# One transformer block on one core: where the second output product's weights are split, and the order of the sums, first MLP weights and norm scalings behind it

## The chip, the core and the metric

The kernel runs on one core of a Trainium2 chip. The metric is the device time in microseconds of one execution. TensorE (PE) does the matmuls, VectorE (DVE), ScalarE (ACT) and GpSimd (POOL) the rest, and SyncE (SP) issues most loads. Each of them works through a queue of its own in order. An instruction that waits therefore holds up everything queued behind it on its engine.

## The reference

One block for 512 tokens of width 1024 in f32: a norm, a wide input projection, two mixers (a gated linear attention with 4 heads and a latent attention with 8), a gated sum of both, the output projection `w_out`, and an MLP of width 4096 with squared relu.

```python
n = rmsnorm(h, g_mix[l])
proj = n @ w_in[l]
...
y_gla = gla_branch(gq, gk, gv, gr, z_gf, z_gb, w_gate_f[l], b_gate_f[l], ...)
y_mla = mla_branch(cq, ckv, kr, positions, g_q[l], w_uq[l], g_kv[l], w_ukv[l])
merged = jax.nn.sigmoid(z_ma) * y_gla + jax.nn.sigmoid(z_mb) * y_mla
h = h + merged @ w_out[l]
m = rmsnorm(h, g_mlp[l])
h = h + jnp.square(jax.nn.relu(m @ w_ff1[l])) @ w_ff2[l]
...
return rmsnorm(h, g_final)
```

Within `mla_branch`, each head computes `p = softmax(q kT)` and then `p v`. This is the "attention" of the text below.

## The kernel before

**Exact products from two halves.** Every f32 operand of a matmul is held as two fp32r tiles, a high part and a low part. `split` makes them: a copy on ACT gives the high tile (names end in `h`), and a subtraction on DVE gives the low tile (names end in `l`). `mm3` then issues three matmuls, high by high, high by low and low by high (L88, L89, L90). In the trace `split` is L93 (ACT) and L94 (DVE), and `split_scaled`, which multiplies by a gain besides, is L97 and L98.

**Attention** is one loop over `n`, over 8 heads (`MH`) of 4 row tiles each, with everything staggered. In step `n`, `att_scores` makes one tile of scores `s` (three matmuls of 512 columns), its row maximum on DVE and the exponential `e` on ACT. `att_normalise` (every second step) divides two tiles by their sums, one on ACT and one on DVE (L1030). `att_flip`, three steps later, transposes a tile on PE into `tp` (four instructions of 128 columns), and splits the result into `pT` (ACT, then DVE). `att_values`, six steps later, makes half a head's values `av` out of `v` and `pT` (12 matmuls of 256 columns), and `merge` gates them. "Transposition 5.2" is head 5, row tile 2. A few loads, splits and sums for the output projection are put into the same loop by the number of the step. Two of these are `streamed(1, ..)` at n = 11, 13 and `streamed(2, ..)` at n = 21, 23. Each loads half of a block of `w_out` into a staging tile (`wf`, of which there are three) and splits it. The tiles are `bo10h`, `bo10l`, `bo11h` and so on, `bo20h`, `bo20l`, `bo21h`, `bo21l` for the second product. In the loop the framework's scheduler chooses the order on PE, ACT and DVE, with a few orders pinned by `goes_behind`.

**Output projection.** The 1024 x 1024 product is done as seven half-sized products in place of eight (a scheme of the Strassen kind), in the order 1, 2, 5, 6, 3, 7, 4. `wo_product(m)` takes the left tiles `wo_left[p][m]` (`gao`, `gdo` and others, which `split_first`, `split_sum` and `corner` make from the merged rows) and the right tiles `wo_right[m]` (`bo{m}0h` and so on, made by `split_part` from blocks `B11`, `B12`, `B21`, `B22` of `w_out`). Sums of those blocks that products 5, 6, 7 and 4 need are formed by loads that add to what lies in the tile (`load_onto`, on GpSimd's queue). Each product has 24 matmuls of 512 columns: four `p`, two row blocks `rb`, three each, except that products 3, 7 and 4 are issued in two halves, one for each `rb`. They write into three pairs of banks: `wox` (products 1, 6, 7, 4), `wow` (2) and `woz` (5, 3). Products 6, 7 and 4 go on adding to `wox`, so that `add_rows`, which adds a bank to the rows `h` on DVE (L1331), reads a bank in the middle of its sums, and the next product on that bank has to wait until it is read.

**Norm and first MLP products.** For rows 0 and 1, and later 2 and 3, `first_half_square` and `second_half_square` sum the squares on ACT, `row_rstd` makes the reciprocal root (one instruction on DVE, one on POOL, `hp`), and `scaled` multiplies the row (one half on DVE, one on ACT, both `ms`). `flipped` transposes the rows on PE, and `evacuate` brings eight banks' parts per half into `mT` (L97 on ACT, L98 on DVE). The first two MLP products `f00` and `f01` take weights that `proj_begin` loads, splits and gives a bank. They run for tokens 0 to 255 first, and after the transpositions of rows 2 and 3 for the others. `f02` follows.

**Order.** From the line `begun = traced()` ahead of the products, `in_program_order(begun, PE_ONLY + SPLITTERS)` pins PE, ACT and DVE to the order in which the program is written, up to the end of the first two MLP products. POOL is pinned so from the start of attention. SP's loads are not pinned in that way, and go where the scheduler puts them: a load waits at its place in SP's queue until the tile that it fills is free. The order of the stage that the change rewrites reads, shortened:

```python
wo_right[4] = split_w2(B21, "bo4")
wo_product(7, (0,))
add_rows(2, 1, xs_[0], ALU.subtract)
first_half_square(2, 1)
...
fm.evacuate(0, range(4))
wo_product(7, (1,), range(2, NP))
add_rows(3, 1, xs_[1], ALU.subtract)
fm.evacuate(0, range(4, KD))
...
early.append(proj_begin(w1, P, "f01", "mm"))
```

Of the kernel before, what the change touches and what calls it, by code (L numbers as in the profile page):

```python
# [18 lines left out]
P = 128  # L19
S = 512  # L20
NT = S // P
D = 1024
KD = D // P
# [33 lines left out]
def tile_block(ctx: ExitStack, tc: tile.TileContext, t, out: bass.AP):  # L57
# [34 lines left out]
    def split(hi, lo, src, rest=nc.vector):  # L92
        nc.scalar.activation(hi, src, AF.Copy)  # L93
        rest.tensor_tensor(lo, src, raw(hi), op=ALU.subtract)  # L94
# [12 lines left out]
    def traced():  # L107
        return len(nc.cur_bb.bb.instructions)
# [16 lines left out]
    def goes_behind(late, early, engines):  # L125

        ins = nc.cur_bb.bb.instructions
        for e in engines:
            a, b = [[i for i in ins[x:y] if i.engine == e] for x, y in (early, late)]
            if a and b:  # L130
                issued_after(b[0], a[-1].name)
# [48 lines left out]
    def row_rstd(parts):  # L180
        nc.vector.scalar_tensor_tensor(
            parts[:, 3:4], parts[:, 1:2], 1.0 / D, parts[:, 2:3], op0=ALU.mult, op1=ALU.add
        )
        nc.gpsimd.tensor_tensor(parts[:, 3:4], parts[:, 3:4], mhalf, op=ALU.pow)
        return parts[:, 3:4]
# [29 lines left out]
    def halves(nk, nw, name):  # L215
        wh = tl([P, nk, nw], F32R, "wh", 4, f"{name}h")
        wl = tl([P, nk, nw], F32R, "wl", 4, f"{name}l")
        return wh, wl
# [12 lines left out]
    def proj_begin(w, col, name, tag="mm"):  # L231
        wh, wl = weights(w[:, col : col + P], name)
        return wh, wl, ps(tag, name)

    def begin_late(col, name, tag="mm"):

        wf = stage(KD, P, name)
        nc.sync.dma_start(wf, w_in[:, col : col + P].rearrange("(k p) w -> p k w", p=P))
        wh, wl = halves(KD, P, name)
        nc.scalar.activation(wh, wf, AF.Copy)  # L240

        def lows():
            nc.vector.tensor_tensor(wl, wf, raw(wh), op=ALU.subtract)

        return (wh, wl, ps(tag, name)), lows
# [654 lines left out]
    def load_w2(qd, x, w=w2, block=None):  # L900

        for g, dst in enumerate(block_tiles(x)):
            for pp_ in range(2):
                nc.sync.dma_start(dst[:, pp_, :], block_rows(w, qd, x if block is None else block, g, pp_))

    def load_onto(dst, x, w):

        for g, d in enumerate(block_tiles(dst)):
            rows = w[4 * g * P : 4 * (g + 1) * P, (x % 2) * S : (x % 2 + 1) * S]
            nc.gpsimd.dma_start(d, rows.rearrange("(k t p) w -> p t k w", t=2, p=P)[:, x // 2], accum_op=ALU.add)  # L910
# [5 lines left out]
    def streamed(m, x, g):  # L916

        wf = stage(2, S, f"bo{m}{g}")
        for pp_ in range(2):
            nc.sync.dma_start(wf[:, pp_, :], block_rows(w_out, 0, x, g, pp_))  # L920
        wh, wl = halves(2, S, f"bo{m}{g}")
        split(wh, wl, wf)
        wo_right.setdefault(m, []).append((wh, wl))

    def split_part(x, g, name):
# [4 lines left out]
    def split_w2(x, name):  # L930
        return [split_part(x, g, name) for g in range(NP // 2)]
# [10 lines left out]
        eng.tensor_tensor(z[:, HT:S], a12, y[:, HT:S], op=ALU.add)  # L942
        return y, z

    merged, wo_right = {}, {}
    wo_left = [{} for _ in range(NP)]
    corners = {}

# [308 lines left out]
    next(units)  # L1257
    attending = traced()
    sums_of, flipping, span = {}, {}, {}
    for n in range(4 * MH + LAG_C):  # L1260
        if n % 2 == 0 and 2 <= n <= 4 * MH:
            att_normalise((n - 2) // 4, (n - 2) % 4)
        scored = traced()
        if n < 4 * MH:
            att_scores(n // 4, n % 4)
            if n - 2 in flipping:
                goes_behind((scored, traced()), flipping[n - 2], SPLITTERS)
        scored = scored, traced()
        if 2 <= n % 8 < 7:
            next(units, None)  # L1270
        if n in (6, 14):
            units = up_units(n // 8 + 2)
            next(units)
        b = n - LAG_B
        if 0 <= b < 4 * MH:
            flips = traced()
            att_flip(b // 4, b % 4)
            flipping[n] = flips, traced()
            if b == 0:
                gla_turn(GH - 1, (flips, traced()))  # L1280

        if n == 20:
            load_onto(B11, B12, w_out)
        extra = traced()
        for x, at in (("y", (18, 26, 34)), ("z", (20, 28, 36))):
            if n in at:
                p = at.index(n)
                to = (5, 6) if x == "y" else (7, 3)
                split_sum(wo_left[p], sums_of[p, x], *to, f"{x}o{p}", nc.gpsimd if p < 2 else nc.vector)
        if n in (19, 30):  # L1290
            p = (19, 30).index(n)
            split_first(wo_left[p], merged[p][0], f"o{p}", nc.gpsimd)
        if n < 4 * MH:
            goes_behind((extra, traced()), scored, SPLITTERS[:1])
        if n == 35:
            split_first(wo_left[2], merged[2][0], "o2")
        if n in (11, 13):
            streamed(1, B11, (n - 11) // 2)
        if n in (21, 23):
            streamed(2, B21, (n - 21) // 2)  # L1300
        if n == 15:
            load_w2(0, B11, w_out)
        if n == 17:
            at = traced()
            load_w2(0, B21, w_out, B22)
            span["sums"] = at, traced()
        if n == 23:
            load_onto(B21, B11, w_out)
        if n == 24:
            load_w2(0, B12, w_out)  # L1310
            load_w2(0, B22, w_out)
        c = n - LAG_C
        if c >= 0 and c % 2 == 1:
            att_values(c // 4, (c % 4) // 2)
        if n == 33:
            load_onto(B21, B12, w_out)
        if c > 0 and c % 8 == 7 and c // 8 < NP - 1:
            sums_of[c // 8, "y"], sums_of[c // 8, "z"] = merged_sums(c // 8, nc.gpsimd)
    load_onto(B12, B22, w_out)

    hrow = []
    for i in range(NT):
# [6 lines left out]
    def add_rows(i, c, acc, op=ALU.add):  # L1329
        hc = hrow[i][:, c * S : (c + 1) * S]  # L1330
        nc.vector.tensor_tensor(hc, hc, acc, op=op)  # L1331
# [3 lines left out]
    def first_half_square(i, c):  # L1335
        hparts[i] = sm(f"hp{i}", 4)
        ms_rows[i] = u4(f"ms{i}", F32, (P, D))
        square_half(hrow[i], c, hparts[i], ms_rows[i], True)

    def second_half_square(i, c):  # L1340
        square_half(hrow[i], c, hparts[i], ms_rows[i], False)

    def scaled(i):
        m = ms_rows[i]
        rs = row_rstd(hparts[i])
        nc.vector.tensor_scalar(m[:, 0:S], hrow[i][:, 0:S], rs, None, op0=ALU.mult)
        nc.scalar.activation(m[:, S:D], hrow[i][:, S:D], AF.Copy, scale=rs)

    def flipped(i):
        fm.rows(i, ms_rows[i])  # L1350
# [140 lines left out]
    def wo_product(m, rbs=range(2), ps_=range(NP)):  # L1491
        accs = wo_accs.get(m, xs_)
        for p in ps_:
            lh, ll = wo_left[p][m]
            wh, wl = wo_right[m][p // 2]
            for rb in rbs:
                tok = slice(rb * P, (rb + 1) * P)
                mm3(accs[rb], lh[:, tok], ll[:, tok], wh[:, p % 2, :], wl[:, p % 2, :],
                    m in (1, 2, 5) and p == 0, p == NP - 1, m not in (1, 2, 5))

    last = NP - 1
    g_last = split_first(wo_left[last], merged[last][0], f"o{last}", nc.vector, None, slice(0, HT))
    wo_product(1)
    wo_right[5] = [split_part(B11, 0, "bo5")]
    split_first(wo_left[last], merged[last][0], f"o{last}", nc.vector, g_last, slice(HT, S))
    y, z = merged_sums(last, nc.vector)
# [30 lines left out]
    for rb in range(2):  # L1537
        wo_product(3, (rb,))
        add_rows(rb, 1, zs_[rb])
        second_half_square(rb, 1)  # L1540
        scaled(rb)
    wo_right[4] = split_w2(B21, "bo4")
    load_w2(0, B21)
    wo_product(7, (0,))
    add_rows(2, 1, xs_[0], ALU.subtract)
    first_half_square(2, 1)
    flipped(0)
    wo_product(7, (1,), range(2))
    flipped(1)
    at = traced()  # L1550
    fm.evacuate(0, range(4))
    wo_product(7, (1,), range(2, NP))
    add_rows(3, 1, xs_[1], ALU.subtract)
    fm.evacuate(0, range(4, KD))
    first_half_square(3, 1)
    span["evacuate", 0] = at, traced()
    at = traced()
    early = [proj_begin(w1, 0, "f00", "mm")]
    goes_behind((at, traced()), span["sums"], SP_ONLY)
    wo_product(4, (0,))  # L1560
    add_rows(2, 0, xs_[0])
    second_half_square(2, 0)
    at = traced()
    early.append(proj_begin(w1, P, "f01", "mm"))
    goes_behind((at, traced()), span["sums"], SP_ONLY)
    wo_product(4, (1,))
    at = traced()
    add_rows(3, 0, xs_[1])
    second_half_square(3, 0)
    for i in (2, 3):  # L1570
        scaled(i)
    span["norm", 3] = at, traced()
    proj_run(early[0], mT, 0)
    proj_run(early[1], mT, 0, range(5))
# [84 lines left out]
```

## Time and profile before

| | |
|---|---|
| three timed runs | 768.16, 768.33 and 768.70 us, median 768.33 |
| profiled execution | 768.7 us, of which the profiled span is 767.0 |
| granted TensorE clock in it | 0.999 |
| attention's second half, output projection, first MLP products | 349 to 438 us of the span |
| first product's end, second product's start | 392.9 us |

The span's clock starts with the first instruction of the profile, so that all places below are given in us from there. An instruction's row gives the start, the duration, the engine, the line of the program, the operation, the tiles out and in, the shape, and in brackets the idle time of the engine just before it with what ended that. A row with "x4" stands for four such instructions together. A row of the windows gives, for a stretch, its length and then the busy time (and count) of PE, PE's weight loads, DVE, ACT and POOL, then the granted clock, the share of the 16 DMA engines and GB/s.

### The profile page before, as it was taken

How to read it: one execution, taken by the hardware profiler on the slowest of the kernel's cores; microseconds unless marked ns; L12 is line 12 of the kernel's file. 1: busy time of each engine (PE TensorE's matmuls, PEld its weight loads, DVE VectorE, ACT ScalarE, POOL GpSimd, SP SyncE). 2: the span in 40 equal slices, each digit the busy share in tenths (PEclk: the TensorE clock that was granted, in tenths of full speed). 3: DMA queues.
4: the chain of work that ended last, by engine and by line, in shares of the span. 5: the costliest groups of instructions: out<-in, count | busy, mean ns of one | idle time of the engine just before them, and what ended most of it. 6: DMA issues, size and time to landing. Idle time of an engine off the chain costs nothing.

```text
span 767.0 us, 10229 instructions
## 1 busy us (share of the span) xinstructions
PE 755.7 (99%) x3744; PEld 637.4 (83%) x3744; DVE 579.7 (76%) x850; ACT 453.5 (59%) x768; POOL 149.6 (20%) x226
## 2 busy tenths in 40 slices
PE   9999999999999999999999999999999999999996
PEld 7888788889888889899888888888888888888885
DVE  7789999756767765999887776965887478848695
ACT  8456668475466555889854766435653555346644
POOL 0720005260624105036761000000000000000014
PEclk9999999999999999999999999999999999999999
DMA  9833211221324325138986421353115510550002
GB/s 315 248 111 108 91 28 28 56 65 46 83 76 114 62 53 134 29 91 209 274 191 182 128 83 55 107 177 102 55 56 177 152 31 26 191 166 1 27 1 109
DMA packets 97185, 81.28 MB, mean 106 GB/s; under 512 B 15504, under 2 KB 74896, under 8 KB 97136
## 3 DMA queue, kind: packets, MB, share of 16 engines
q1 hardware_dynamic: 93904, 74.33, 32.6%
q0 software_dynamic: 2944, 6.03, 4.2%
q8 instruction: 29, 0.48, 0.3%
q10 hardware_dynamic: 288, 0.28, 0.1%
q14 instruction: 20, 0.16, 0.1%
HBM read 76.96 MB, written 2.10 MB: 103 GB/s over the span
## 4 chain that ended last, share of the span: by engine, by line
PE 91%; DVE 4%; ACT 3%; issue 1%; POOL 0%; DMA 0%; POOLq 0%; SPq 0%; ACTq 0%; DVEq 0%
PE f L89 7%; PE f L90 7%; PE f L88 7%; PE gx L88 4%; PE gx L90 4%; PE gx L89 4%; PE first L327 3%; PE za L88 2%; PE za L89 2%; PE gz L88 2%; PE za L90 2%; PE gz L89 2%; PE gz L90 2%; PE zb L88 1%; PE zb L90 1%; PE zb L89 1%
## 5 line engine op out<-in xcount | busy, mean ns | idle before, releaser
L1598 POOL DMA_DIRECT2D gfin<-in_g_final x1 | 0.6, 622 | 283.0 <-PE f L90 283.0
L914 DVE TENSOR_TENSOR w<-w,w 128x1024 f32<-128x1024 f32 x32 | 38.7, 1220 | 0.3
L475 POOL COPY v3f<-rrf 128x4 f32<-128x4 f32 x4 | 2.8, 708 | 135.9 <-DVE rrf L458 135.9
L1023 ACT ACTIVATE e<-s,top 128x512 f32<-128x512 f32 x32 | 22.0, 688 | 6.3 <-DVE top L1018 5.2
L94 DVE TENSOR_TENSOR pT<-tp,pT 128x512 fp32r<-128x512 f32 x32 | 21.5, 681 | 2.3 <-ACT pT L93 2.1
L1331 DVE TENSOR_TENSOR h<-h,gx 128x512 f32<-128x512 f32 x32 | 21.5, 681 | 1.9 <-PE gx L90 1.8
L1018 DVE TENSOR_REDUCE top<-s 128x1 f32<-128x512 f32 x32 | 21.6, 681 | 1.1 <-PE s L90 0.7
L93 ACT ACTIVATE pT<-tp 128x512 fp32r<-128x512 f32 x32 | 18.6, 596 | 2.7 <-PE tp L1038 2.5
L1038 PE MATMUL tp<-ident,e 128*128 128x128 f32 x128 | 19.3, 274 | 0.3 <-ACT e L1029 0.2
L88 PE MATMUL av<-pT,v 128*128 128x256 f32 x64 | 19.1, 298 | 0.4 <-ACT pT L93 0.4
L89 PE MATMUL av<-pT,v 128*128 128x256 f32 x64 | 18.4, 288 | 0.4 <-DVE pT L94 0.4
L1398 ACT ACTIVATE fa<-f 128x512 f32<-128x512 f32 x32 | 18.5, 577 | 0.0
L93 ACT ACTIVATE ghb<-y 128x512 fp32r<-128x512 f32 x16 | 10.1, 633 | 14.0 <-DVE y L860 14.0
L90 PE MATMUL av<-pT,v 128*128 128x256 f32 x64 | 18.2, 285 | 0.0
L94 DVE TENSOR_TENSOR sc<-sc,sc 128x512 fp32r<-128x512 f32 x16 | 10.9, 690 | 9.5 <-ACT sc L93 9.5
L1038 PEld LDWEIGHTS tp<-ident,e 128*128 128x128 f32 x128 | 15.0, 141 | 3.0 <-ACT e L1029 0.7
L93 ACT ACTIVATE sc<-sc 128x512 fp32r<-128x512 f32 x16 | 9.3, 596 | 11.5 <-DVE sc L546 11.5
L88 PE MATMUL s<-kbuf,q 96*128 96x512 f32 x32 | 14.3, 446 | 0.4 <-DVE pT L94 0.4
L93 ACT ACTIVATE b_00h<-w 128x1024 fp32r<-128x1024 f32 x7 | 7.4, 1060 | 12.3 <-PE gx L90 6.0
L93 ACT ACTIVATE b_10h<-w 128x1024 fp32r<-128x1024 f32 x7 | 7.4, 1059 | 12.1 <-PE gz L90 6.0
L93 ACT ACTIVATE b_20h<-w 128x1024 fp32r<-128x1024 f32 x7 | 7.4, 1059 | 12.1 <-PE gz L90 6.0
L1407 ACT ACTIVATE px<-fa 128x256 f32<-128x256 f32 x32 | 13.4, 418 | 1.0
(1667 smaller groups left out, 2930.3 us busy)
## 6 DMA issues: line engine op xcount, KB each, us to landing
w<-in_w_ff SPq DMA_DIRECT2D x64, 256.0 KB, 3.3
w<-in_w_out POOLq DMA_DIRECT2D x10, 512.0 KB, 8.0
grw<-in_w_in SPq DMA_DIRECT2D x8, 512.0 KB, 8.6
gvw<-in_w_in SPq DMA_DIRECT2D x8, 512.0 KB, 4.7
w<-in_w_out SPq DMA_DIRECT2D x16, 256.0 KB, 4.7
x<-in_xt SPq DMA_DIRECT2D x8, 256.0 KB, 5.2
vw<-in_w_first SPq DMA_DIRECT2D x8, 256.0 KB, 5.3
h<-in_x SPq DMA_DIRECT2D x4, 512.0 KB, 6.7
```

What stands on the lines that cost most here:

```text
L88: nc.tensor.matmul(acc, lh, rh, start=start, stop=False, skip_group_check=onto)
L89: nc.tensor.matmul(acc, lh, rl, start=False, stop=False, skip_group_check=onto)
L90: nc.tensor.matmul(acc, ll, rh, start=False, stop=stop, skip_group_check=onto)
L93: nc.scalar.activation(hi, src, AF.Copy)
L94: rest.tensor_tensor(lo, src, raw(hi), op=ALU.subtract)
L327: nc.tensor.matmul(f_accs[i], a[:, i * P : (i + 1) * P], b, start=k == 0 and x == 0, stop=k == KD - 1 and x == 2)
L914: nc.vector.tensor_tensor(wq[dst][g], wq[x][g], wq[y][g], op=op)
L1018: nc.vector.tensor_reduce(top, acc, axis=AX.X, op=ALU.max, negate=True)
L1023: nc.scalar.activation(e, acc, AF.Exp, bias=top, accum_out=tot[:, qt % 2 : qt % 2 + 1])
L1038: nc.tensor.transpose(tp[:, k * P : (k + 1) * P], e[:, k * P : (k + 1) * P], ident)
L1331: nc.vector.tensor_tensor(hc, hc, acc, op=op)
L1398: nc.scalar.activation(a, acc, AF.Relu)
```

## The change

Nothing is computed otherwise. The change moves instructions:

- `streamed` only loads its staging tile, and `split_streamed` splits it. For the first product both stand together as before. For the second, the splits move out of attention (n = 21, 23): one to just ahead of the first product, one behind it.
- The attention loop ends one step earlier. What that step held, the last values `att_values(MH - 1, 1)`, now stands in the program in the middle of the first product, and `load_onto(B12, B22, w_out)` behind it.
- The fourth product's weights `bo4` are split in two parts, with the first sum behind the seventh product (`add_rows(2, 1, ..)`) between them.
- `f00` is begun before the squares of row 2, and the eight evacuations of the first half stand together, behind the second sum of the seventh product.
- `f01` is begun by `begin_late`, which holds the low part back: the load and the high part stand ahead of the fourth product, the low part behind the last squares of row 3.
- `row_rstd` for row 2 comes ahead of row 3's last squares, for row 3 behind `f01`'s low part. The scalings of both rows stand last.

```diff
--- before.py
+++ after.py
@@ -232,10 +232,10 @@
         wh, wl = weights(w[:, col : col + P], name)
         return wh, wl, ps(tag, name)
 
-    def begin_late(col, name, tag="mm"):
+    def begin_late(col, name, tag="mm", w=None):
 
         wf = stage(KD, P, name)
-        nc.sync.dma_start(wf, w_in[:, col : col + P].rearrange("(k p) w -> p k w", p=P))
+        nc.sync.dma_start(wf, (w_in if w is None else w)[:, col : col + P].rearrange("(k p) w -> p k w", p=P))
         wh, wl = halves(KD, P, name)
         nc.scalar.activation(wh, wf, AF.Copy)
 
@@ -919,7 +919,11 @@
         for pp_ in range(2):
             nc.sync.dma_start(wf[:, pp_, :], block_rows(w_out, 0, x, g, pp_))
         wh, wl = halves(2, S, f"bo{m}{g}")
-        split(wh, wl, wf)
+        streams[m, g] = wf
+
+    def split_streamed(m, g):
+        wh, wl = halves(2, S, f"bo{m}{g}")
+        split(wh, wl, streams.pop((m, g)))
         wo_right.setdefault(m, []).append((wh, wl))
 
     def split_part(x, g, name):
@@ -942,7 +946,7 @@
         eng.tensor_tensor(z[:, HT:S], a12, y[:, HT:S], op=ALU.add)
         return y, z
 
-    merged, wo_right = {}, {}
+    merged, wo_right, streams = {}, {}, {}
     wo_left = [{} for _ in range(NP)]
     corners = {}
 
@@ -1257,7 +1261,7 @@
     next(units)
     attending = traced()
     sums_of, flipping, span = {}, {}, {}
-    for n in range(4 * MH + LAG_C):
+    for n in range(4 * MH + LAG_C - 1):
         if n % 2 == 0 and 2 <= n <= 4 * MH:
             att_normalise((n - 2) // 4, (n - 2) % 4)
         scored = traced()
@@ -1296,6 +1300,7 @@
             split_first(wo_left[2], merged[2][0], "o2")
         if n in (11, 13):
             streamed(1, B11, (n - 11) // 2)
+            split_streamed(1, (n - 11) // 2)
         if n in (21, 23):
             streamed(2, B21, (n - 21) // 2)
         if n == 15:
@@ -1316,7 +1321,6 @@
             load_onto(B21, B12, w_out)
         if c > 0 and c % 8 == 7 and c // 8 < NP - 1:
             sums_of[c // 8, "y"], sums_of[c // 8, "z"] = merged_sums(c // 8, nc.gpsimd)
-    load_onto(B12, B22, w_out)
 
     hrow = []
     for i in range(NT):
@@ -1340,9 +1344,8 @@
     def second_half_square(i, c):
         square_half(hrow[i], c, hparts[i], ms_rows[i], False)
 
-    def scaled(i):
+    def scaled(i, rs):
         m = ms_rows[i]
-        rs = row_rstd(hparts[i])
         nc.vector.tensor_scalar(m[:, 0:S], hrow[i][:, 0:S], rs, None, op0=ALU.mult)
         nc.scalar.activation(m[:, S:D], hrow[i][:, S:D], AF.Copy, scale=rs)
 
@@ -1500,7 +1503,12 @@
 
     last = NP - 1
     g_last = split_first(wo_left[last], merged[last][0], f"o{last}", nc.vector, None, slice(0, HT))
-    wo_product(1)
+    split_streamed(2, 0)
+    wo_product(1, ps_=(0, 1))
+    att_values(MH - 1, 1)
+    load_onto(B12, B22, w_out)
+    wo_product(1, ps_=(2, 3))
+    split_streamed(2, 1)
     wo_right[5] = [split_part(B11, 0, "bo5")]
     split_first(wo_left[last], merged[last][0], f"o{last}", nc.vector, g_last, slice(HT, S))
     y, z = merged_sums(last, nc.vector)
@@ -1538,37 +1546,39 @@
         wo_product(3, (rb,))
         add_rows(rb, 1, zs_[rb])
         second_half_square(rb, 1)
-        scaled(rb)
-    wo_right[4] = split_w2(B21, "bo4")
-    load_w2(0, B21)
+        scaled(rb, row_rstd(hparts[rb]))
+    wo_right[4] = [split_part(B21, 0, "bo4")]
     wo_product(7, (0,))
     add_rows(2, 1, xs_[0], ALU.subtract)
+    wo_right[4].append(split_part(B21, 1, "bo4"))
+    load_w2(0, B21)
+    flipped(0)
+    at = traced()
+    early = [proj_begin(w1, 0, "f00", "mm")]
+    goes_behind((at, traced()), span["sums"], SP_ONLY)
     first_half_square(2, 1)
-    flipped(0)
     wo_product(7, (1,), range(2))
     flipped(1)
-    at = traced()
-    fm.evacuate(0, range(4))
     wo_product(7, (1,), range(2, NP))
     add_rows(3, 1, xs_[1], ALU.subtract)
-    fm.evacuate(0, range(4, KD))
+    fm.evacuate(0)
     first_half_square(3, 1)
-    span["evacuate", 0] = at, traced()
     at = traced()
-    early = [proj_begin(w1, 0, "f00", "mm")]
+    begun_f, lows = begin_late(P, "f01", "mm", w1)
+    early.append(begun_f)
     goes_behind((at, traced()), span["sums"], SP_ONLY)
     wo_product(4, (0,))
     add_rows(2, 0, xs_[0])
     second_half_square(2, 0)
-    at = traced()
-    early.append(proj_begin(w1, P, "f01", "mm"))
-    goes_behind((at, traced()), span["sums"], SP_ONLY)
     wo_product(4, (1,))
     at = traced()
     add_rows(3, 0, xs_[1])
+    rs2 = row_rstd(hparts[2])
     second_half_square(3, 0)
-    for i in (2, 3):
-        scaled(i)
+    lows()
+    rs3 = row_rstd(hparts[3])
+    scaled(2, rs2)
+    scaled(3, rs3)
     span["norm", 3] = at, traced()
     proj_run(early[0], mT, 0)
     proj_run(early[1], mT, 0, range(5))
```

## The prediction

> **What bounds the kernel now.** I read the page first: TensorE is busy for all but 11 us, and the chain that ended last is nearly all matmuls. So nothing can be won by making another engine do less; only places where TensorE stands still count.
>
> ```profile
> PE 755.7 (99%) x3744; PEld 637.4 (83%) x3744; DVE 579.7 (76%) x850; ACT 453.5 (59%) x768; POOL 149.6 (20%) x226
> ...
> PE 91%; DVE 4%; ACT 3%; issue 1%; POOL 0%; DMA 0%; POOLq 0%; SPq 0%; ACTq 0%; DVEq 0%
> ```
>
> Next the windows, by stage. The change touches the second half of attention, the output projection and the norm behind it. Two stretches of 20 us there have idle TensorE time, 1.22 us (end of attention) and 1.24 us (last products, norm, first MLP products):
>
> ```profile
> 365.00:385.00 20.00, 18.78 (x129) 16.56 (x128) 17.03 (x33) 16.62 (x37) 15.09 (x17) 1.00 0.96 287
> 418.00:438.00 20.00, 18.76 (x115) 15.61 (x114) 13.36 (x23) 13.41 (x28) 1.48 (x4) 1.00 0.35 106
> ```
>
> Then the timeline of TensorE around those idles. Matmuls overlap, so a stop costs more than the idle that is shown; the distance of starts tells it. Attention:
>
> ```profile
> 364.93 0.60 PE L1038 MATMUL tp<-ident,e 128*128 128x128 f32 x4
> 365.29 0.36 PE L88 MATMUL av<-pT,v 128*128 128x256 f32 x1
> ...
> 365.73 0.28 PE L88 MATMUL av<-pT,v 128*128 128x256 f32 x1
> 366.45 0.50 PE L88 MATMUL s<-kbuf,q 96*128 96x512 f32 x1 [0.44 <-DVE pT L94]
> ```
>
> Fourth product, first MLP products:
>
> ```profile
> 424.37 0.39 PE L89 MATMUL wox<-bo41l,gdo 128*128 128x512 f32 x1
> 424.60 0.39 PE L90 MATMUL wox<-bo41h,gdo 128*128 128x512 f32 x1
> 425.33 0.50 PE L88 MATMUL wox<-bo40h,gdo 128*128 128x512 f32 x1 [0.34 <-DVE h L1331]
> ...
> 431.15 0.28 PE L88 MATMUL f<-mT,f01h 128*128 128x256 f32 x1
> 431.27 0.28 PE L89 MATMUL f<-mT,f01h 128*128 128x256 f32 x1
> 431.97 0.38 PE L90 MATMUL f<-mT,f01l 128*128 128x256 f32 x1 [0.43 <-DVE f01l L94]
> ...
> 437.14 0.39 PE L88 MATMUL f<-mT,f02h 128*128 128x512 f32 x1
> 437.85 0.38 PE L89 MATMUL f<-mT,f00h 128*128 128x256 f32 x1 [0.31 <-DVE mT L98]
> ```
>
> A 512-column matmul starts 0.23 after the one before, a 256-column one 0.12. So these stops cost 0.72-0.12 = 0.60 in attention, and 0.73-0.23 = 0.50, 0.70-0.12 = 0.58, 0.71-0.23 = 0.48 in the norm. Summing start distance less regular distance over the 129 and the 115 matmuls of the two windows gives 2.5 and 2.3 us; the rest are gaps too short to carry a bracket. That 4.8 us is all the change can win.
>
> **Part 1: the second product's weights.** `streamed(2, ..)` at n=21 and 23 loses its two splits; they come back as `split_streamed(2, ..)` around the first product. Removed from attention: two ACT copies and two DVE subtractions of 128x1024, of which one is
>
> ```profile
> 363.85 1.35 DVE L94 TENSOR_TENSOR bo21l<-bo21f,bo21h 128x1024 fp32r<-128x1024 f32 x1
> ```
>
> This ends at 365.2; the reduction and the `pT` subtraction queued behind it are what the scores at 366.45 wait for. That 0.60 goes with it. The later gaps come indirectly: the built program has another order there. From head 4 on, `av` stands in whole blocks, the score groups come earlier, and each transposition is asked for after its normalisation. I laid the after order along TensorE by hand, with 0.70 per score group (three of 0.23), 0.36 per transposition (364.93 to 365.29 above) and 0.12 per `av` matmul, and ACT and DVE instructions at the traced lengths, from 349 us on, where the orders part. No place stops TensorE for certain, but four transpositions (5.2, 6.0, 6.2, 7.0) are ready within 0.1 us of being asked for. I count one stop of 0.60 for them and so 1.9 of 2.5; from below, all 2.5; from above, none, if every tight place slips.
>
> These tight places hang on DVE, whose lengths vary with GpSimd's work beside it: a normalisation takes 0.81 beside two GpSimd sums and 0.48 alone.
>
> ```profile
> 370.62 0.81 DVE L1030 TENSOR_SCALAR e<-e,tot 128x512 f32<-128x512 f32 x1
> ...
> 376.78 0.48 DVE L1030 TENSOR_SCALAR e<-e,tot 128x512 f32<-128x512 f32 x1
> ```
>
> The Trainium skill ("SBUF — State Buffer", Who interferes with whom) says that VectorE and GpSimd lock one pair of ports for a whole instruction, and that whoever comes first blocks the other. The two rows agree. The rule speaks against a full gain here: no GpSimd instruction leaves attention. By the rule alone each tight place would slip by 0.81-0.48 = 0.33, and nearly all of the 1.9 would be lost to four restarts; by the row of 0.48 only those that meet a sum. It raises the chance of case (a) below.
>
> Where the splits land, they lie in idle time. ACT stands 3.14 us before `bo50h`; the second product starts 2.5 us after that:
>
> ```profile
> 390.33 1.06 ACT L93 ACTIVATE bo50h<-w 128x1024 fp32r<-128x1024 f32 x1 [3.14 <-PE wox L90]
> ```
>
> ```profile
> 392.86 0.39 PE L88 MATMUL wow<-bo20h,gao 128*128 128x512 f32 x1
> ```
>
> Two copies of 1.06 fit into 3.14. DVE in the same place:
>
> ```profile
> 387.93 0.68 DVE L94 TENSOR_TENSOR glzo<-zo,ghzo 128x512 fp32r<-128x512 f32 x1
> ```
>
> This ends at 388.6. Then come the lows of half of `mx3` (0.4, half of such a row and a little), `bo20l` (1.35 at the long end: 390.4, wanted at 392.86), the last merge (0.4) and `bo21l` (392.2, wanted by the thirteenth matmul of the second product, 12 x 0.23 = 2.8 after 392.86). The cost is nothing; without that cover it would be 2 x 1.35. `bo50l`, `yo3` and what is queued behind them come later by a few tenths, and the third product that wants them starts 24 x 0.23 = 5.5 after 392.86.
>
> `att_values(7, 1)` and the loads of `B12` onto which `B22` is added keep their place in GpSimd's queue: zero. The last values now stand whole between the halves of the first product, while before the scheduler put them there itself: zero. `streamed` still claims two tiles that nothing writes; no instruction comes of it.
>
> Staging buffers: `bo20f` and `bo21f` hold two of three until the splits, so `f01f` and `f02f` move on SP's queue from ahead of the `B12`, `B22` and `x` loads to behind them. Behind those two wait the MLP's second weights. They gain nothing and lose nothing unless the transfers collide: that stretch is full.
>
> ```profile
> 388.00:412.00 24.00, 24.00 (x113) 20.03 (x112) 20.18 (x31) 12.26 (x19) 8.17 (x9) 1.00 1.07 237
> ```
>
> TensorE is busy for all 24.00, so no transfer is late now, though the queues are full (1.07). Two loads of 128x1024 f32, 1.05 MB, are 4.4 us more at this row's 237 GB/s. The cost lies between zero and 4.4. I take zero: the products here wait for no transfer and are 2 us apart, and the `x` rows and both `w_out` loads get clear of the two loads that SP held in front of them.
>
> **Part 2: sums of the seventh product.** Before:
>
> ```profile
> 420.05 1.22 DVE L94 TENSOR_TENSOR bo41l<-w,bo41h 128x1024 fp32r<-128x1024 f32 x1
> 421.19 0.68 DVE L1331 TENSOR_TENSOR h<-h,wox 128x512 f32<-128x512 f32 x1
> 423.02 1.66 DVE L98 SCALAR_TENSOR_TENSOR mT<-mb,gvec,mT 128x256 fp32r<-128x256 f32 x4 [1.15 <-ACT mT L97]
> 424.60 0.68 DVE L1331 TENSOR_TENSOR h<-h,wox 128x512 f32<-128x512 f32 x1
> ...
> 430.69 1.23 DVE L94 TENSOR_TENSOR f01l<-f01f,f01h 128x1024 fp32r<-128x1024 f32 x1 [1.74 <-ACT f01h L93]
> 431.84 0.68 DVE L1331 TENSOR_TENSOR h<-h,wox 128x512 f32<-128x512 f32 x1
> ```
>
> The second sum waits behind four evacuations, and TensorE waits for its bank. New DVE order: `bo40l`, sum (420.05), `bo41l` (420.65), `f00l` (421.8; its copy on ACT, 1.04 like `f02h` below, has until then), sum (422.95 to 423.6), eight evacuations (to 426.8, as now). The fourth product's second half wants its bank at 424.7: 0.50 goes, 1.1 to spare; the first half's short wait goes too.
>
> **Part 3: first MLP weights and scalings.** `f01h` now stands before the squares of row 2, so `f01l` no longer waits 1.74 for it: it ends near 429.6, wanted at 430.8 on the shifted clock. 0.58 goes. The rows' chain:
>
> ```profile
> 422.53 3.01 ACT L97 ACTIVATE mT<-mb,gvec 128x256 fp32r<-128x256 f32 x8
> ...
> 434.47 0.72 ACT L1347 ACTIVATE ms<-h,hp 128x512 f32<-128x512 f32 x1 [0.49 <-POOL hp L184]
> 435.10 1.04 ACT L93 ACTIVATE f02h<-f02f 128x1024 fp32r<-128x1024 f32 x1
> ```
>
> From the last sum (431.84) to the last scaling (434.47) is 2.63. The last sum moves to 427.8, so the scaling starts by 430.4 and `f02h` by 431.1. TensorE wants the scaled rows at 432.4: the short gaps there go. `f02l` ends at 433.4, and the first evacuation behind it at 434.3, wanted at 435.2: the 0.48 goes. Evacuations (0.38 each, 3.01/8) then outrun the matmuls (six of 0.12). What is late next: nothing before the product. I take 2.2 of 2.3; from above zero, if `f00l` ahead of the evacuations delayed them by its 1.2, which 428.2 covers.
>
> **Sum.** 1.9 + 2.2 = 4.1. The profiled execution took 768.7 (span 767.0, 1.7 around it): 764.6. The median of the runs is 768.33, 0.37 lower: 764.2.
>
> **Rivals.** (a) Attention is DVE-bound after all and new gaps replace the old: DVE is busy 17.03 of 20 us there, which speaks for it; that the splits are gone, against. Only the norm's 2.2 remains: 766.1. (b) The norm's gains fail, because `f00l` and `bo41l` ahead of the sums only exchange one queue for another; against it the spare 1.1 at each step. 1.9 remains: 766.4. (c) Both stages make new gaps of the same size, or the change doesn't do what it says because TensorE's order around it is nearly the same: 768.3. (d) Slower: `av` blocks standing whole no longer fill the waits of the transpositions, and DVE becomes the pace of the end of attention. From transposition 5.2 on there are ten transpositions and eight blocks, 18 places where TensorE can wait for DVE. With n stops of 0.60 in place of the 2.5, the time changes by 0.6n - 2.5 - 2.2: even at eight, slower beyond noise from eleven, 2.5 over at twelve, 770.8. For it: DVE's 85%, which leaves 3 us in 20. Against: only 2.5 us of stops in that window now, 0.60 of it with the splits as its cause.
>
> (e) The moved `f01f` and `f02f` hold up the adding loads of GpSimd's queue in the full stretch, by all of 4.4 us, and the product that reads them waits: 764.2 + 4.4 = 768.6. The 24.00 of 24.00 says that there is a margin, not how large. The Trainium skill ("DMA: Bandwidth & Descriptors", Issuing engines are not separate DMA queues) says that transfers from all issuing engines interleave on the same 16 DMA engines. By that the moved loads can't pass beside the others; the row's 1.07 agrees that there is no room.
>
> **Numbers.** Forecast 0.64 (763.2 to 765.3), (a) 0.16, (b) 0.05, (c) 0.06, (d) 0.06, (e) 0.03. The measurement tells 0.2%, 1.5 us, from no change. Faster takes the forecast, (a) and 0.03 of (b): 0.83. Same takes (c), (e) and the rest of (b): 0.11. Slower is (d): 0.06. The range begins where all 4.8 are gone and a run falls 0.3 below the median (763.2); it ends 0.5 beyond (b) (766.9), and leaves out (c), (d) and (e), 0.15.
>
> **What would show it.** Right: TensorE without brackets in the 20 us up to the first MLP products, and at most one or two among the last transpositions; DVE and ACT busy where ACT stood 3.14; the second product 2 us earlier. Wrong: brackets of 0.3 to 0.4 on `tp` or `av` from head 5 on, a wait for `bo20l`, or a DMA named before `bo60h`, `bo70h` or `bo40h`.

## The result, and the profile after

The changed kernel takes 763.22 us (median of 6 runs, 762.79 to 764.05). The kernel before takes 768.22 beside it (768.15 to 768.70). The ratio is 0.9936, with a 95% interval from 0.9924 to 0.9949. It is 5.0 us faster, where 4.1 were forecast.

The page first: TensorE (PE) has the same 3744 matmuls, busy for all but 9 us of a shorter span, and the chain that ended last holds more matmuls and less VectorE (DVE) and ScalarE (ACT) than before.

```profile
PE 752.1 (99%) x3744; PEld 636.1 (84%) x3744; DVE 580.7 (76%) x850; ACT 453.3 (60%) x768; POOL 150.5 (20%) x226
...
PE 97%; DVE 1%; ACT 1%; issue 0%; POOL 0%; POOLq 0%; ACTq 0%
```

The windows, for the three stretches that the prediction showed (the columns are the same: length, then the busy time of PE, PE's loads, DVE, ACT, POOL, the clock, the DMA share, GB/s):

```profile
365.00:385.00 20.00, 19.89 (x142) 17.90 (x141) 17.41 (x34) 17.85 (x40) 16.22 (x19) 1.00 0.82 247
388.00:412.00 24.00, 24.00 (x107) 19.86 (x106) 22.11 (x34) 12.02 (x20) 7.51 (x8) 1.00 1.09 259
418.00:438.00 20.00, 20.00 (x144) 18.82 (x142) 15.11 (x28) 13.65 (x30) 2.58 (x4) 1.00 0.51 140
```

The 1.22 and 1.24 us of idle PE are 0.11 and 0 now. DVE is no less busy in the first window than before (17.41 against 17.03): of the subtractions that left attention, only the last 0.2 us of `bo21l` (363.85 to 365.20) lay in it, and what stays is done in less time.

Where the time went is read from the distance between the same matmuls in both traces. Rows of PE's timeline in the kernel before:

```profile
347.98 0.39 PE L90 MATMUL uq<-cqhl,wq3l 128*128 128x512 f32 x1
...
760.12 0.28 PE L90 MATMUL gend<-b_31h,ga 128*128 128x256 f32 x1
```

and after:

```profile
347.16 0.39 PE L90 MATMUL uq<-cqhl,wq3l 128*128 128x512 f32 x1
...
389.86 0.39 PE L88 MATMUL wow<-bo20h,gao 128*128 128x512 f32 x1
...
424.28 0.28 PE L88 MATMUL f<-mT,f00h 128*128 128x256 f32 x1
...
754.17 0.28 PE L90 MATMUL gend<-b_31h,ga 128*128 128x256 f32 x1
```

At 348 us the profiled execution after is 0.82 ahead already, before PE meets anything that has changed. This lead is there at 15 us and hardly moves until 348. Over all fourteen traces the same matmul of the first product starts between 15.12 and 16.19 us; why is open. The two profiled executions are besides the slowest of one kernel's first three and the fastest of the other's six. So all that follows is measured from this matmul on. From there to the second product's first matmul it is 44.88 us before (347.98 to 392.86) and 42.70 after: **2.18 won in attention** (stage A). From there to the last matmul it is 367.26 and 364.31: **2.95 won behind it** (stage N). Together that is 5.13, and the medians differ by 5.0. The starts of products 5, 6, 3 and 7 follow at equal distances in both, to 0.01 us. Nearly all of stage N's gain, 2.81, is there at 443.6 us of the kernel before: in the sums, the norm and the first MLP products.

### The profile page after: what moved, and what is told of

Its sections match the earlier page's. It is cut to its first block, busy times and chain, and to the rows that moved or that the text cites. A ratio compares the mean times of both kernels' runs of the same rounds, so it can differ in the third digit from the quotient of the medians.

```text
span 761.0 us, 10233 instructions
## 1 busy us (share of the span) xinstructions
PE 752.1 (99%) x3744; PEld 636.1 (84%) x3744; DVE 580.7 (76%) x850; ACT 453.3 (60%) x768; POOL 150.5 (20%) x226
## 4 chain that ended last, share of the span: by engine, by line
PE 97%; DVE 1%; ACT 1%; issue 0%; POOL 0%; POOLq 0%; ACTq 0%
PE f L88 8%; PE f L89 8%; PE f L90 8%; PE gx L88 4%; PE gx L90 4%; PE gx L89 4%; PE first L327 3%; PE tp L1042 2%; PE za L88 2%; PE za L89 2%; PE za L90 2%; PE gz L88 2%; PE gz L90 2%; PE gz L89 2%; PE zb L88 1%; PE zb L90 1%
```

## The experiments

Each experiment is read twice: its timed median (5 to 10 runs, beside runs of the kernel before with medians of 768.27 to 768.53), and stages A and N of its trace, as above (won against the kernel before). A stage can be read to some 0.1 us: in the six kernels that change only attention against the changed one, or nothing, N lies between 2.81 and 2.94. The medians are coarser, since they hold the difference of the first 16 us too.

| kernel | median, us | ratio, 95% interval | A | N |
|---|---|---|---|---|
| changed | 763.22 | 0.9924 to 0.9949 | 2.2 | 2.9 |
| part 1 alone | 766.58 | 0.9965 to 0.9985 | 2.1 | 0.1 |
| splits alone | 766.82 | 0.9971 to 0.9989 | 2.0 | -0.1 |
| parts 2 and 3 alone | 765.63 | 0.9951 to 0.9976 | 0.0 | 2.8 |
| changed, subtractions also in attention | 763.52 | 0.9923 to 0.9950 | 1.7 | 2.8 |
| changed, copies also in attention | 763.40 | 0.9922 to 0.9949 | 2.0 | 2.8 |
| changed, both also in attention | 764.45 | 0.9936 to 0.9961 | 1.2 | 2.9 |
| changed, attention in the order before | 764.72 | 0.9942 to 0.9967 | 0.7 | 2.9 |
| both in attention, order after | 765.03 | 0.9945 to 0.9972 | 0.3 | 2.9 |
| changed, `f01` as before | 764.83 | 0.9940 to 0.9965 | 2.1 | 1.7 |
| changed, `bo4` whole | 764.34 | 0.9931 to 0.9956 | 2.2 | 2.5 |
| changed, evacuations as before | 764.72 | 0.9938 to 0.9963 | 2.2 | 2.0 |
| changed, `f00` as before | 763.43 | 0.9922 to 0.9947 | 2.1 | 2.6 |

### Each part alone

Part 1 alone is the kernel before with these edits, the splits alone only the two marked lines with the new `streamed`:

```diff
-    for n in range(4 * MH + LAG_C):
+    for n in range(4 * MH + LAG_C - 1):
...
-    load_onto(B12, B22, w_out)
...
-    wo_product(1)
+    split_streamed(2, 0)        # splits alone
+    wo_product(1, ps_=(0, 1))
+    att_values(MH - 1, 1)
+    load_onto(B12, B22, w_out)
+    wo_product(1, ps_=(2, 3))
+    split_streamed(2, 1)        # splits alone
```

> The kernel before with part 1 alone (second product's splits moved behind the probabilities, the last values and the adding load inside the first product). Theory (the two stages lose their stops independently): the traces of before and after put 2.2 us of the gain ahead of the second product, so this kernel takes 768.2 - 2.2 = 766.0, and the stops of the norm (0.50, 0.58, 0.48 and the short ones) stay. Rival (the norm's stops come from what attention leaves late, so that part 1 alone removes them too, or the gain of attention is eaten by a longer wait at the norm): 763.2 or 768.2.

> The kernel before with only the splits of the second product moved; the last values and the adding load of B12 stay where they were. TensorE's order in attention is then that of the changed kernel. Theory (the move of the splits makes all of the gain there): 766.0, as part 1 whole, within 0.3. Rival (the shorter loop, with the last values between the halves of the first product, is needed): 767 or more, with a stop at the last av or between the first and second product.

> The kernel before with parts 2 and 3 alone (fourth product's weights in two parts, sums, f00, f01, scalings in the new sequence). Theory: 2.8 us, what the two traces differ by from the seventh product on, so 765.4, with attention's stops as before. Rival (the new sequence needs the head start that attention gives, or only works with the loads of f01 and f02 moved on SP's queue): less than half, above 766.8.

The stages are independent: each part wins its own stage and nothing in the other, and 2.17 and 2.81 over the whole distance add up to the 5.13 within 0.2. The timed gains, 1.7 and 2.6, are 0.7 short of 5.0 in sum, no more than the intervals allow; the medians of part 1 and of the splits alone, 766.58 and 766.82, are also 0.6 and 0.8 above the 766.0 expected. The shorter loop matters little: the splits alone win 2.0 of 2.1 in A. They lose 0.3 at one place, where the stop ahead of the fourth product is longer; that loss is gone with the last values moved too. Why was not followed up.

### Work or order: attention

The changed program differs in attention in two things: four instructions are gone from ACT and DVE, and the scheduler, without them, gives all three engines another order. Three kernels put work back into tiles that nothing reads:

```diff
         wh, wl = halves(2, S, f"bo{m}{g}")
         streams[m, g] = wf
+        if m == 2:
+            nc.vector.tensor_tensor(wl, wf, wf, op=ALU.subtract)   # subtractions
+            nc.scalar.activation(wh, wf, AF.Copy)                  # or: copies
+            split(wh, wl, wf)                                      # or: both
```

> The changed kernel with two subtractions of 128x1024 on VectorE put back where the second product's splits stood in attention (they write tiles that nothing reads), ScalarE as changed. Theory (VectorE's queue holds the reductions and the pT subtractions of which TensorE waits, so that its 2 x 1.2 us there are the cause of attention's stops): most of attention's 2.2 us comes back, 764.7 to 765.4, with brackets that name DVE. Rival (ScalarE's copies are the cause, or both engines have slack): 763.2 to 763.6.

> The changed kernel with the two copies of 128x1024 on ScalarE alone left in attention; TensorE's order is exactly that of the changed kernel. Theory A (ScalarE has room there, 17 busy us of 20): 763.2 to 763.6. Theory B (the copies of 1.06 us hold the exponentials and the pT copies behind them, and are the cause of attention's stops): 764.5 to 765.5.

> The changed kernel with both halves of the second product's splits (two copies on ScalarE, two subtractions on VectorE behind them) also left where they stood in attention, writing tiles that nothing reads. The scheduler then gives TensorE a third order, neither that of before nor that of the changed kernel. Theory (the split work in attention makes the stops): most of the 2.2 us comes back, 764.9 to 765.6. Rival (the stops were those of the order that the scheduler happened to choose around the splits, and not of their work, of which two subtractions alone cost 0.5 us): 763.2 to 764.2.

The copies cost 0.2 in A (theory A), the subtractions alone 0.5, less than half of what I expected; their 763.52 lies where the rival put it. But the scheduler put these subtractions earlier than the splits had stood, as they wait for no copy; DVE's timeline of that kernel has them at 349 and 356, not at 364:

```profile
349.10 1.49 DVE L924 TENSOR_TENSOR bo20l<-bo20f 128x1024 fp32r<-128x1024 f32 x1 [0.18 <-issue]
...
356.41 1.20 DVE L924 TENSOR_TENSOR bo21l<-bo21f 128x1024 fp32r<-128x1024 f32 x1
```

So that run says little about the place that the prediction named. With both halves back the second subtraction stands where it stood before, and the stop that the prediction read is there again, in the DVE and PE timelines:

```profile
363.30 1.34 DVE L94 TENSOR_TENSOR bo21l<-bo21f,bo21h 128x1024 fp32r<-128x1024 f32 x1
364.56 0.68 DVE L1024 TENSOR_REDUCE top<-s 128x1 f32<-128x512 f32 x1
365.16 0.68 DVE L94 TENSOR_TENSOR pT<-tp,pT 128x512 fp32r<-128x512 f32 x1
```

```profile
365.89 0.50 PE L88 MATMUL s<-kbuf,q 96*128 96x512 f32 x1 [0.47 <-DVE pT L94]
```

Yet A loses only 1.0 of its 2.2: the scheduler made a third order around this work, and the later stops of the kernel before are short in it. Two more kernels therefore part the work from the order. One is the changed kernel, with attention's instructions chained on PE, ACT and DVE in the order of the kernel before (without the splits). The other is the kernel with both halves back, chained in the changed kernel's order:

```diff
+    for e, runs in wanted.items():      # runs: the order wanted, for PE, ACT, DVE
+        own = [i for i in nc.cur_bb.bb.instructions[attending:] if i.engine == e and i.name not in spare]
+        order = [own[k] for a, b in runs for k in range(a, b)]
...
+        for i, j in zip(order, order[1:]):
+            issued_after(j, i.name)
```

> The changed kernel, its splits moved, with the instructions of attention on TensorE, ScalarE and VectorE pinned to the order in which the kernel before has them (the splits left out of it). Theory (work: the split work in attention makes a part of the stops, about 1.0 of 2.2 us as the kernel with both splits left in showed, and the order that the scheduler chose around them the rest): about 1.2 us is lost up to the second product, 764.4, with the stops at 373.1 and 382.2 of before still there and the one at 366.45 gone. Rival 1 (the order costs nothing once the work is gone): 763.2. Rival 2 (the order alone makes all): 765.4, with the stop at 366.45 too.

> The reverse: both halves of the second product's splits left in attention as well (writing tiles that nothing reads), and attention's other instructions pinned to the changed kernel's order on TensorE, ScalarE and VectorE. Theory (work and order each make a part): 0.6 to 1.0 us is lost up to the second product, 763.9 to 764.3, with one stop of 0.4 to 0.6 behind the second split. Rival 1 (order alone): 763.2 to 763.4. Rival 2 (work alone): 765.4.

Without the work but in the order before, the stop at 366.45 is gone and the other two stand as they stood. PE in the kernel before:

```profile
373.12 0.39 PE L88 MATMUL av<-pT,v 128*128 128x256 f32 x1 [0.36 <-ACT pT L93]
...
382.17 0.38 PE L89 MATMUL av<-pT,v 128*128 128x256 f32 x1 [0.35 <-DVE pT L94]
```

and in this kernel:

```profile
371.79 0.39 PE L88 MATMUL av<-pT,v 128*128 128x256 f32 x1 [0.35 <-ACT pT L93]
...
380.84 0.39 PE L89 MATMUL av<-pT,v 128*128 128x256 f32 x1 [0.36 <-DVE pT L94]
```

A wins 0.7: that is what taking the work out is worth by itself, the stop of 0.60 and the 0.10 that the next matmul starts late behind it (366.45 to 366.78, 0.33 in place of 0.23). With the work in but in the new order, A wins 0.3, and the stops are new ones, ahead of transpositions 4.3, 5.0 and 5.2; PE's timeline:

```profile
360.87 0.66 PE L1047 MATMUL tp<-ident,e 128*128 128x128 f32 x4 [0.16 <-ACT e L1032]
...
363.20 0.63 PE L1047 MATMUL tp<-ident,e 128*128 128x128 f32 x4 [0.96 <-DVE pT L94]
...
367.32 0.66 PE L1047 MATMUL tp<-ident,e 128*128 128x128 f32 x4 [0.23 <-ACT e L1038]
```

In this kernel, however, the split of `bo21` does not stand where it stood in the kernel before. The chains hold attention's own instructions only, and the copy of `bo21` runs at 356.81 (361.63 before), its subtraction on DVE at 358.30 (363.85 before):

```profile
358.30 1.21 DVE L94 TENSOR_TENSOR bo21l<-bo21f,bo21h 128x1024 fp32r<-128x1024 f32 x1
```

So neither does it alone: 0.7 by the work, 0.3 by the order (with the split at this earlier place), 2.2 by both. What the new order would lose with the split at 363.85 no run shows, nor which engine's order counts. The new order asks for its transpositions so early that it holds only where ACT and DVE have room: with the split in, DVE runs without an idle bracket from 350.2 to 366.0, and all three stops name ACT or DVE. My theory that both make a part is right for the first kernel (1.5 lost, 1.2 expected) and fails for the second: 1.9 lost where I expected 0.6 to 1.0.

### The sums, `f00`, `f01`

Four kernels undo one edit of parts 2 and 3 each. The evacuations and the fourth product's weights:

```diff
     flipped(1)
+    fm.evacuate(0, range(4))            # evacuations as before
     wo_product(7, (1,), range(2, NP))
     add_rows(3, 1, xs_[1], ALU.subtract)
-    fm.evacuate(0)
+    fm.evacuate(0, range(4, KD))
```

> The changed kernel with the second sum of the seventh product behind four of the eight evacuations again, as before. Theory (the sum's place behind the evacuations made the stop of 0.50 before the fourth product's second half): 0.5 to 0.6 us lost ahead of the first MLP product, and up to 0.3 behind it, 763.7 to 764.1, with a bracket on wox that names DVE h. Rival (the two subtractions ahead of it set that sum, not the evacuations): 763.2 to 763.4.

```diff
-    wo_right[4] = [split_part(B21, 0, "bo4")]
+    wo_right[4] = split_w2(B21, "bo4")  # bo4 whole
+    load_w2(0, B21)
     wo_product(7, (0,))
     add_rows(2, 1, xs_[0], ALU.subtract)
-    wo_right[4].append(split_part(B21, 1, "bo4"))
-    load_w2(0, B21)
```

> The changed kernel with the fourth product's weights split in one piece ahead of the seventh product, so that the first sum on VectorE stands behind bo41l again. The second sum still stands ahead of the evacuations. Theory (the stops at the fourth product came from the sum behind four evacuations, not from the one behind bo41l): 0 to 0.15 us, 763.2 to 763.4. Rival (the first sum's delay of 1.2 us is what TensorE waited for): 0.5 us and more, 763.7.

The second sum behind four evacuations brings back the stop that the prediction named, on PE. On the way to the first MLP product 0.82 is lost, more than the 0.5 to 0.6 that I expected, and 0.1 behind it:

```profile
421.54 0.39 PE L90 MATMUL wox<-bo41h,gdo 128*128 128x512 f32 x1
422.44 0.50 PE L88 MATMUL wox<-bo40h,gdo 128*128 128x512 f32 x1 [0.52 <-DVE h L1335]
422.78 0.39 PE L89 MATMUL wox<-bo40l,gdo 128*128 128x512 f32 x1
```

The sum behind `bo41l` costs 0.32 there and 0.4 in all of N. That is between the theory (up to 0.15) and the rival (0.5 and more), and nearer to the rival; its timed median, 764.34, is on the rival's side. In the trace the loss begins again ahead of a product that adds to the bank (PE's timeline, 0.42 between starts in place of 0.23):

```profile
418.94 0.39 PE L90 MATMUL wox<-bo71h,glco 128*128 128x512 f32 x1
419.36 0.47 PE L88 MATMUL wox<-bo40h,gdo 128*128 128x512 f32 x1
```

The first MLP weights:

```diff
-    begun_f, lows = begin_late(P, "f01", "mm", w1)
-    early.append(begun_f)
...
     second_half_square(2, 0)
+    early.append(proj_begin(w1, P, "f01", "mm"))   # f01 as before
     wo_product(4, (1,))
...
-    lows()
```

> The changed kernel with f01 begun as before, its load, copy and subtraction together behind the squares of row 2. Theory: the stop before the first f01l product (0.58 before) comes back whole or in part, since the copy again stands behind the squares and the subtraction behind it: 763.7 to 764.0, with a bracket on f that names DVE f01l. Rival (the earlier last sum alone has moved everything forward far enough): 763.2 to 763.4.

```diff
-    early = [proj_begin(w1, 0, "f00", "mm")]
     first_half_square(2, 1)
...
     first_half_square(3, 1)
+    early = [proj_begin(w1, 0, "f00", "mm")]       # f00 as before
```

> The changed kernel with f00 begun where it was before, behind the squares of row 3, just ahead of f01. Theory (f00's low part has its place ahead of the evacuations, and behind them ends 1.0 to 1.5 us after TensorE asks for it; f01's copy is pushed back by the same 1.05): 1.0 to 1.5 us lost, 764.2 to 764.7, with a bracket on the first f. Rival (the copy and the subtraction find idle time there): 763.2 to 763.6.

`f01` as before costs 1.2 in N, more than the 0.5 to 0.8 expected, and not where I expected it: the first `f01l` product is in time, by 0.1 (`f01l` ends at 428.09, the product starts at 428.19), since everything stands earlier. The last sum on DVE waits behind `f01l` (428.00) and the scalings behind it, so that PE waits for the scaled row and then for the evacuations:

```profile
426.86 1.23 DVE L94 TENSOR_TENSOR f01l<-f01f,f01h 128x1024 fp32r<-128x1024 f32 x1 [1.74 <-ACT f01h L93]
428.00 0.68 DVE L1335 TENSOR_TENSOR h<-h,wox 128x512 f32<-128x512 f32 x1
...
430.55 0.49 DVE L1349 TENSOR_SCALAR ms<-h,hp 128x512 f32<-128x512 f32 x1 [0.44 <-POOL hp L184]
```

```profile
430.25 1.94 PE L199 MATMUL mb<-ident,ms 128*128 128x128 f32 x16 [0.30 <-DVE ms L1349]
...
433.93 0.39 PE L89 MATMUL f<-mT,f00h 128*128 128x256 f32 x1 [0.30 <-DVE mT L98]
```

`f00` as before costs 0.3, not the 1.0 to 1.5 that I expected: its 763.43 is where the rival put it. Without `f00h` and `f00l` ahead of them the evacuations are done 0.8 earlier on both engines, counted from the matmul at 347 us, and `f00l` takes that time behind them:

```profile
419.87 3.22 DVE L98 SCALAR_TENSOR_TENSOR mT<-mb,gvec,mT 128x256 fp32r<-128x256 f32 x8
423.62 1.23 DVE L94 TENSOR_TENSOR f00l<-f00f,f00h 128x1024 fp32r<-128x1024 f32 x1 [0.53 <-ACT f00h L93]
```

It ends at 424.85, and PE starts its first matmul with `f00l` at 424.90, 0.29 behind the one before in place of 0.12, and the next 0.22 behind that: these two make the 0.3. In stage N the evacuations, `bo4`, `f01` and `f00` make 0.9, 0.4, 1.2 and 0.3: nearly the 2.9. None of these kernels was faster than the changed one; in attention one stop of 0.27 us is left.

## Why the prediction was right

**The bound.** Right: stops of PE were what was to be won, and all but 0.1 of the gain came from the two windows that it named. But "all the change can win" was put at 4.8, and 5.0 was won (5.13 in the traces). The measured 763.22 lies 0.02 above the lower end of the range, 763.2. That end was drawn from the 4.8 and 0.3 for noise, not from the term that turned out larger. That the time fell inside was luck, though the mechanism was right.

**Part 1.** Forecast 1.9, measured 2.2. The stop of 0.60 hangs on the split of `bo21`: it is gone without the work and back with it. The later stops "come indirectly", by the order: shown by the pinned kernel, which keeps them. What the prediction did not see is how much work and order need each other. It treated the tight transpositions as a matter of 0.60, while the new order with work left in loses 1.9, two of its three stops at transpositions that the prediction had not counted (4.3 and 5.0). Where it allowed for one stop of 0.60, there is one of 0.27 in the changed kernel, ahead of transposition 6.0:

```profile
369.54 0.28 PE L89 MATMUL av<-pT,v 128*128 128x256 f32 x1
369.93 0.63 PE L1042 MATMUL tp<-ident,e 128*128 128x128 f32 x4
```

It is not the wait that the prediction feared, for ACT had normalised that tile by 368.15. What it waits for carries no bracket, and stays open. So 1.9 came near 2.2 with an allowance for a wait that did not occur.

**Where the splits landed.** Right: `bo20l` ends at 388.41, 1.45 ahead of the product that starts at 389.86, and no stop stands there. The forecast had 2.5 to spare (390.4 for 392.86), so the split came 1.0 later against its product than laid out. DVE's timeline after:

```profile
387.20 1.21 DVE L94 TENSOR_TENSOR bo20l<-bo20f,bo20h 128x1024 fp32r<-128x1024 f32 x1
...
388.67 1.21 DVE L94 TENSOR_TENSOR bo21l<-bo21f,bo21h 128x1024 fp32r<-128x1024 f32 x1
389.81 1.76 DVE L94 TENSOR_TENSOR bo50l<-w,bo50h 128x1024 fp32r<-128x1024 f32 x1
```

**The moved loads** cost nothing, as taken: PE is busy for 24.00 of 24.00 us in the full stretch, with the queues at 1.09 of their time where they were at 1.07. Rival (e) is out.

**Parts 2 and 3.** Each step holds, but the term is mis-sized: 2.2 forecast, 2.8 to 2.9 measured. DVE's timeline after has the second sum, `f01l` and `f02l`:

```profile
419.95 0.68 DVE L1335 TENSOR_TENSOR h<-h,wox 128x512 f32<-128x512 f32 x1
...
425.33 1.23 DVE L243 TENSOR_TENSOR f01l<-f01f,f01h 128x1024 fp32r<-128x1024 f32 x1
...
429.32 1.23 DVE L94 TENSOR_TENSOR f02l<-f02f,f02h 128x1024 fp32r<-128x1024 f32 x1 [1.27 <-ACT f02h L93]
```

With the 3.00 us that this trace is ahead (392.86 against 389.86) they end at 423.6, 429.6 and 433.6 of the clock before, where 423.6, 429.6 and 433.4 were forecast. The sum of 2.3 was not over all matmuls of the window, as the prediction has it: it is what the distances make that are more than 0.1 over the regular one, and all of them come to 2.6 (2.9 if those below the regular one are not counted against it). So it left out what follows a stop: the first matmul behind it is itself slow, and the next one starts late. The kernel before, behind its stop of 0.50 at the fourth product:

```profile
425.33 0.50 PE L88 MATMUL wox<-bo40h,gdo 128*128 128x512 f32 x1 [0.34 <-DVE h L1331]
425.67 0.40 PE L89 MATMUL wox<-bo40l,gdo 128*128 128x512 f32 x1
```

The distance is 0.34 in place of 0.23, so this stop costs 0.1 more than its own gap. Matmul against matmul, the stops that the change removes in N come to 2.2, as forecast. At the matmuls behind four of them the changed kernel gains another 0.08, 0.12, 0.10 and 0.11, together 0.4, and the remaining 0.3 comes in steps of 0.06 and less, of which no run shows the cause.

**The rivals.** (a) would leave 2.2 only; A's 2.2 are there. (b) fails with N's 2.9, (c) with both, (d) since only one short stop stands where it counted eighteen places. Its mechanism is real, though: with split work left in and the new order, A is nearly back at the kernel before.

## What to carry to other kernels

When a scheduler chooses the order, a moved instruction is two changes: its own time, and another order of all that stays. Build both and pin the order to tell them apart, and look where the work that was put back has landed; here either alone was worth a third or less. Where an engine reads a bank in the middle of a sum, put that read ahead of everything that can wait: here four evacuations in front of it cost 0.9 us, and one subtraction 0.4. And when stops are counted in a stream of matmuls, count starts, and add the slow start behind each one.

## What the runs showed of the hardware

Behind a stop PE lost about 0.1 us more here: the next matmul started 0.34 behind the first in place of 0.23, and elsewhere 0.33 in place of 0.23 and 0.22 in place of 0.12.

Additions on GpSimd (POOL) and subtractions on DVE hold each other up here by whole instructions. The changed kernel, POOL's timeline, an addition beside DVE's subtractions, and the same kind of addition at 369:

```profile
369.38 0.77 POOL L1073 TENSOR_TENSOR my<-tb,za 128x256 f32<-128x256 f32 x1
...
388.83 1.66 POOL L1073 TENSOR_TENSOR my<-tb,za 128x256 f32<-128x256 f32 x1 [1.84 <-DVE tb L1070]
```

The addition begins while `bo21l` (388.67 to 389.88) runs, and ends 0.61 behind it, at 390.49. Then `bo50l`, begun at 389.81, takes 1.76 where `bo21l` took 1.21: it ends 1.08 behind the addition. That is one behind the other, in the order in which they came. The Trainium skill ("SBUF — State Buffer", Who interferes with whom) says that a DVE instruction with two SBUF inputs and a GpSimd instruction that reads SBUF share ports, and that the one issued first blocks the other. The trace agrees. What the prediction made of that rule, a delay of 0.33 at each tight transposition, did not come: the last three normalisations on DVE took 0.48, 0.52 and 0.49, though POOL was busy beside two of them (those at 376.87 and 380.13). It was POOL's additions begun during these two that took longer, 0.92 and 0.95 against 0.74 and 0.73 for the ones ahead:

```profile
376.37 0.74 POOL L1073 TENSOR_TENSOR mx<-tb,za 128x256 f32<-128x256 f32 x1 [0.51 <-DVE tot L1032]
377.06 0.92 POOL L1073 TENSOR_TENSOR my<-tb,za 128x256 f32<-128x256 f32 x1
...
379.57 0.73 POOL L945 TENSOR_TENSOR zo<-mx,my 128x256 f32<-128x256 f32 x1
380.27 0.95 POOL L946 TENSOR_TENSOR zo<-mx,yo 128x256 f32<-128x256 f32 x1
```

The two rows that the prediction set side by side are not the whole picture either: in the kernel before, the normalisation at 367.79 took 0.48 with an addition of POOL (367.24 to 367.99) beside it. And the tight transpositions 5.2, 6.0, 6.2 and 7.0 read tiles that ACT normalises (`att_normalise` gives the even row tiles to ACT), so that a longer normalisation on DVE could reach them only through DVE's queue.
